# Pinning the order of the ahead-of-time block sums in a one-core decoder layer

## The chip, the cores and the metric

The kernel runs on one core of a Trainium2 chip, in one launch. The metric is the device time of that core in microseconds: 1126.95 us is the median of three runs (1126.46 to 1127.5). Lower is better.

## The reference

One layer of a decoder, in float32, for 256 tokens of width 2048:

- `h = rmsnorm(x)`, then one projection to q, k, v of 16 heads of 128 (8 stick-breaking heads, 8 dilated-window heads with rotary positions);
- attention of each head, its own RMS norm, concatenation, `mix_out = mixed @ w_out`, and `x = x + rmsnorm(mix_out)`;
- `h = rmsnorm(x)`, `u = h @ w_up` (2 x 5504 columns), a causal depthwise convolution of width 3, `y = gelu(gate) * val`, `f = y @ w_down` (5504 rows), and `x = x + rmsnorm(f)`.

For 26 blocks of the last product (13 pairs of row tiles, two column halves) the kernel uses a two-by-two block scheme with fewer products, which needs sums of blocks of `w_down`. These sums depend on the weights alone, so a part of them is made long before `w_down` is multiplied.

## The kernel before, in words

**Chunks.** The weights pass through TensorE in chunks of 128 x 2048 floats, listed in `chunks`: 0 to 7 are v, 8 to 23 q and k of heads 0 to 7 (two chunks a head), 24 to 27 v, 28 to 35 heads 8 to 11, 36 to 39 v, 40 to 47 heads 12 to 15, 48 to 63 the output projection, and from 64 on the up projection. One loop goes over them (L688). Iteration i first calls `ahead(i)`, which loads chunk i+2 in two halves (L78, into one of five `raw` buffers) and splits chunk i+1 into a high part `wh` (ScalarE, L88) and a low part `wl` (VectorE, L93). Then TensorE multiplies chunk i (L101 and L104 for q and k; L134, L135, L138 for v and the output projection). Then `step()` advances every active head by one stage.

**Heads.** A stick-breaking head's second stage makes scores `z` and ends with `spl` on VectorE (L352). Its third stage, one chunk later, multiplies `spl` (L355). A dilated head first rotates q and k (L364 to L368), and its scores (L372, L373) come one chunk later. They are reduced by L378 and L380. `finish_head` normalises a head's output (L316 to L325 on VectorE).

**Block sums ahead of up.** `presum` (L531) is called at the end of iterations 7 to 61 with `tick = i - 7`. At even ticks it stores the sum of pair `tick/2 - 2` to DRAM (L537, from the tile `t13`), and loads the two blocks of pair `tick/2` (L546 into `b12`, two buffers, 256 KB; L548 into `t13`, three buffers, 512 KB). At odd ticks it adds the blocks of pair `(tick-1)/2 - 1` (L542, VectorE). So in the source pair p is loaded in iteration 7+2p, added in iteration 10+2p and stored in iteration 11+2p. The sums are read back in the down projection, after chunk 149.

**What sets the order.** All these loads and stores are issued by SyncE, in one queue with the `raw` loads. A planner orders the instructions of each engine when the program is built. It follows the source as its priority, but lets an instruction pass others that are, by its own model, not ready or waiting for a buffer. `keep_in_program_order` ties one instruction behind the one that the source gave to the same engine just before it. It does not tie the instructions that follow. The helper `pin` (L65) uses it for whole stretches, as around L745 to L843; `presum` does not use it.

Of the kernel before, what the change touches and what calls it, by code (L numbers as in the profile page):

```python
# [13 lines left out]
ALU = mybir.AluOpType  # L14
# [37 lines left out]
def layer_kernel(ctx: ExitStack, tc: tile.TileContext, a, out: bass.AP):  # L52
    nc = tc.nc
    V, A, T, G = nc.vector, nc.scalar, nc.tensor, nc.gpsimd
# [433 lines left out]
    class Down:  # L488
# [42 lines left out]
        def presum(self, tick):  # L531


            pair, odd = divmod(tick, 2)
            if not odd and 0 <= pair - 2 < len(self.presums):
                t13, _, kept = self.summed[pair - 2]
                nc.sync.dma_start(kept, t13)  # L537
            if odd and 0 <= pair - 1 < len(self.presums):
                t13, one, _ = self.summed[pair - 1]
                b12 = one.rearrange("p (o c) -> p o c", o=1).broadcast_to([P, 2, 512])  # L540
                two = t13.rearrange("p (o c) -> p o c", o=2)
                V.tensor_tensor(two, b12, two, op=ALU.add)  # L542
            if not odd and pair < len(self.presums):
                one, two, kept = self.presums[pair]
                b12 = apool.tile([P, 512], F32, tag="b12", name="b12")
                nc.sync.dma_start(b12, one)  # L546
                t13 = apool.tile([P, HALF], F32, tag="t13", name="t13", bufs=3)
                nc.sync.dma_start(t13, two)  # L548
                self.summed.append((t13, b12, kept))

        def load(self, n):
# [394 lines left out]
```

## Time and profile before

| | |
|---|---|
| median of three runs | 1126.95 us |
| the profiled execution's own time | 1126.68 us |
| its span | 1124.8 us |
| TensorE busy | 1106.9 us |
| VectorE busy | 880.2 us |
| ScalarE busy | 659.4 us |
| mean DMA traffic | 229 GB/s |

The span is the stretch from the first to the last recorded instruction. Busy times are sums over an engine's instructions. Matmuls overlap, so their single durations are longer than the distance between two starts. An idle time stands beside the instruction that ended it, with what released that instruction.

### The profile page before, as it was taken

Reading aid. Unit: us, or ns where it says so; the run is one execution under the profiler, and the core shown is the slowest. Engines: PE = TensorE matmul, PEld = TensorE weight load, DVE = VectorE, ACT = ScalarE, POOL = GpSimd, SP = SyncE. Lnnn points to the kernel's source line nnn. Section 1 sums busy time; section 2 is a strip of 40 time slices with the busy share of each in tenths; the row PEclk is TensorE's granted clock in tenths of the full one; section 3 lists DMA queues with packets and bytes.
Section 4 is the critical chain, followed back from the end, with each engine's and each line's share of the span. In section 5 each row is a group of like instructions: output and inputs, shape, how many; then the busy total and the mean of one; then the engine's idle time right before and its main releaser. Section 6 shows DMA issues by size and latency. Waiting matters only on the chain.

```text
span 1124.8 us, 16273 instructions
## 1 busy us (share of the span) xinstructions
PE 1106.9 (98%) x5855; PEld 942.9 (84%) x5855; DVE 880.2 (78%) x1370; ACT 659.4 (59%) x1038; POOL 3.3 (0%) x10
## 2 busy tenths in 40 slices
PE   9999999999999989999999999999999999999997
PEld 6888888888888878888888888888888888888885
DVE  6577776786765478888888888888888798889887
ACT  6656565565654466555555555555555566666664
POOL 0000000000000000000000000000000000000000
PEclk9999999999999999999999999999999999999998
DMA  9978898998645546555555555555555577767776
GB/s 345 340 279 268 295 351 291 321 329 304 220 167 187 192 172 216 188 188 187 188 188 187 187 188 188 187 187 187 188 187 187 162 260 242 254 217 247 243 246 207
DMA packets 74817, 257.79 MB, mean 229 GB/s; under 512 B 8432, under 2 KB 9328, under 8 KB 73968
## 3 DMA queue, kind: packets, MB, share of 16 engines
q1 hardware_dynamic: 74448, 256.68, 68.4%
q8 instruction: 46, 0.75, 0.3%
q14 instruction: 35, 0.29, 0.1%
q10 hardware_dynamic: 288, 0.07, 0.0%
HBM read 238.89 MB, written 17.83 MB: 228 GB/s over the span
## 4 chain that ended last, share of the span: by engine, by line
PE 93%; DVE 2%; DMA 2%; ACT 1%; issue 1%; SPq 0%; DVEq 0%; ACTq 0%
PE mmu L101 28%; PE mmu L104 14%; PE mmqk L101 9%; PE p L590 7%; PE p L589 6%; PE p L588 6%; PE mmqk L104 4%; PE mmo L134 3%; PE mmo L135 3%; PE mmo L138 3%; PE mmv L138 3%; PE mmv L134 3%; PE mmv L135 3%; DVE wl L93 1%; DMA b<-in_w_dn 1%; DMA t<-in_w_dn 1%
## 5 line engine op out<-in xcount | busy, mean ns | idle before, releaser
L88 ACT CAST wh<-raw 128x1024 fp32r<-128x1024 f32 (+1 forms) x413 | 419.3, 1022 | 359.8 <-PE mmu L101 191.3
L93 DVE TENSOR_TENSOR wl<-raw,wh 128x1024 fp32r<-128x1024 f32 (+1 forms) x413 | 486.8, 1186 | 158.6 <-ACT wh L88 156.2
L101 PE MATMUL mmu<-hT,wh 128*128 128x512 f32 x1344 | 340.6, 395 | 0.2 <-ACT wh L88 0.2
L101 PEld LDWEIGHTS mmu<-hT,wh 128*128 128x128 f32 x1344 | 240.8, 188 | 45.0 <-ACT wh L88 0.4
L104 PEld LDWEIGHTS mmu<-hT,wl 128*128 128x128 f32 x1344 | 184.1, 188 | 15.3
L104 PE MATMUL mmu<-hT,wl 128*128 128x256 f32 x1344 | 187.3, 281 | 0.0
L101 PE MATMUL mmqk<-hT,wh 128*128 128x512 f32 x512 | 132.9, 401 | 0.0
L101 PEld LDWEIGHTS mmqk<-hT,wh 128*128 128x128 f32 x512 | 92.0, 188 | 17.2
L104 PEld LDWEIGHTS mmqk<-hT,wl 128*128 128x128 f32 x512 | 69.9, 188 | 5.8
L590 PE MATMUL p<-wl,yp 128*128 128x512 f32 x182 | 71.8, 395 | 0.0
L589 PE MATMUL p<-wh,yp 128*128 128x512 f32 x182 | 71.4, 392 | 0.0
L104 PE MATMUL mmqk<-hT,wl 128*128 128x256 f32 x512 | 71.1, 281 | 0.0
L588 PE MATMUL p<-wh,yp 128*128 128x512 f32 x182 | 70.6, 388 | 0.0
L590 PE MATMUL p<-wl,yt 128*128 128x512 f32 (+1 forms) x140 | 54.1, 387 | 0.0
L589 PE MATMUL p<-wh,yt 128*128 128x512 f32 (+1 forms) x140 | 53.9, 385 | 0.0
L588 PE MATMUL p<-wh,yt 128*128 128x512 f32 (+1 forms) x140 | 53.4, 382 | 0.0
L461 ACT ACTIVATE cv<-u,par 128x256 f32<-128x256 f32 x86 | 51.5, 599 | 2.6 <-DVE u L459 2.5
L134 PE MATMUL mmv<-wh,hT 128*128 128x512 f32 x128 | 51.4, 403 | 0.8 <-ACT wh L88 0.4
L135 PE MATMUL mmv<-wh,hT 128*128 128x512 f32 x128 | 50.7, 396 | 0.2 <-DVE hT L239 0.2
L134 PE MATMUL mmo<-wh,mix 128*128 128x512 f32 x128 | 50.4, 394 | 0.0
L542 DVE TENSOR_TENSOR t<-b,t 128x1024 f32<-128x1024 f32 x26 | 31.8, 1222 | 23.1 <-DMA t<-in_w_dn 23.0
L135 PE MATMUL mmo<-wh,mix 128*128 128x512 f32 x128 | 49.9, 390 | 0.0
(175 smaller groups left out, 1209.5 us busy)
## 6 DMA issues: line engine op xcount, KB each, us to landing
raw<-in_w_up SPq DMA_DIRECT2D x172, 512.0 KB, 4.1
raw<-in_w_qk SPq DMA_DIRECT2D x64, 512.0 KB, 5.4
raw<-in_w_dn SPq DMA_DIRECT2D x60, 512.0 KB, 4.5
raw<-in_w_o SPq DMA_DIRECT2D x32, 512.0 KB, 3.5
raw<-in_w_v SPq DMA_DIRECT2D x31, 512.0 KB, 5.8
t<-in_w_dn SPq DMA_DIRECT2D x26, 512.0 KB, 6.5
t_kept<-t SPq DMA_DIRECT2D x26, 512.0 KB, 6.8
raw<-t_kept SPq DMA_DIRECT2D x26, 512.0 KB, 4.3
```

The lines of the kernel that those rows point to most:

```text
L88: pin(A.copy(wh, raw))
L93: pin(V.tensor_tensor(wl, raw, wh.bitcast(F32), op=ALU.subtract))
L101: T.matmul(ps, wh[:, j * P:(j + 1) * P], h[:, k, :, :], start=(k == 0), stop=False, skip_group_check=True)
L104: T.matmul(ps[:, 0, :], wl[:, j * P:(j + 1) * P], h[:, k, 0, :], start=False, stop=(k == KT - 1), skip_group_check=True)
L134: T.matmul(ps[t], hi[:, k, tc_], ws, start=(first and i == 0 and j == 0), stop=False)
L135: T.matmul(ps[t], lo[:, k, tc_], ws, start=False, stop=False)
L138: T.matmul(ps[t], hi[:, k, tc_], wl[:, j * 512:(j + 1) * 512], start=False, stop=(last and i == len(parts) - 1 and j == n - 1))
L461: A.activation(cv, u, AF.Identity, scale=cw(2), bias=par[:, P_CB + f:P_CB + f + 1])
L542: V.tensor_tensor(two, b12, two, op=ALU.add)
L588: T.matmul(ps, yh, wh[:, cs], start=key not in self.begun, stop=False)
L589: T.matmul(ps, yl, wh[:, cs], start=False, stop=False)
L590: T.matmul(ps, yh, wl[:, cs], start=False, stop=self.left[key] == 0)
```

## The change

The five instructions of `presum` that move or add blocks are each given to `keep_in_program_order`. Nothing is added, removed or resized. Each is tied behind the instruction that the source placed just before it on its engine (SyncE for the three DMAs, VectorE for the addition).

```diff
@@ -534,18 +534,18 @@
             pair, odd = divmod(tick, 2)
             if not odd and 0 <= pair - 2 < len(self.presums):
                 t13, _, kept = self.summed[pair - 2]
-                nc.sync.dma_start(kept, t13)
+                tc.keep_in_program_order(nc.sync.dma_start(kept, t13))
             if odd and 0 <= pair - 1 < len(self.presums):
                 t13, one, _ = self.summed[pair - 1]
                 b12 = one.rearrange("p (o c) -> p o c", o=1).broadcast_to([P, 2, 512])
                 two = t13.rearrange("p (o c) -> p o c", o=2)
-                V.tensor_tensor(two, b12, two, op=ALU.add)
+                tc.keep_in_program_order(V.tensor_tensor(two, b12, two, op=ALU.add))
             if not odd and pair < len(self.presums):
                 one, two, kept = self.presums[pair]
                 b12 = apool.tile([P, 512], F32, tag="b12", name="b12")
-                nc.sync.dma_start(b12, one)
+                tc.keep_in_program_order(nc.sync.dma_start(b12, one))
                 t13 = apool.tile([P, HALF], F32, tag="t13", name="t13", bufs=3)
-                nc.sync.dma_start(t13, two)
+                tc.keep_in_program_order(nc.sync.dma_start(t13, two))
                 self.summed.append((t13, b12, kept))
```

## Rows read from the trace of the kernel before

**Rows 1.** The page: span, and busy time of each engine.
```profile
span 1124.8 us, 16273 instructions
PE 1106.9 (98%) x5855; PEld 942.9 (84%) x5855; DVE 880.2 (78%) x1370; ACT 659.4 (59%) x1038; POOL 3.3 (0%) x10
```
**Rows 2.** Windows: stretch, length, busy times, clock, DMA share, GB/s.
```profile
50.00:100.00 50.00, 50.00 (x296) 43.97 (x295) 37.27 (x63) 29.44 (x56) 0.00 (x0) 1.00 0.79 272
100.00:150.00 50.00, 48.98 (x292) 43.02 (x291) 36.96 (x66) 28.46 (x61) 0.00 (x0) 1.00 0.90 308
150.00:175.00 25.00, 23.36 (x128) 19.69 (x127) 18.86 (x34) 14.76 (x33) 0.00 (x0) 1.00 0.95 335
...
200.00:225.00 25.00, 24.18 (x143) 20.78 (x143) 18.46 (x40) 15.26 (x32) 0.00 (x0) 1.00 0.92 321
225.00:250.00 25.00, 24.57 (x134) 20.94 (x133) 21.29 (x47) 15.59 (x37) 0.00 (x0) 1.00 0.92 323
...
325.00:350.00 25.00, 25.00 (x118) 20.76 (x117) 12.32 (x18) 11.44 (x18) 0.00 (x0) 1.00 0.53 172
```
**Rows 3.** Waits of PE: who waited for whom, total us, times, longest.
```profile
PE z L355 <- DVE spl L352: 2.7, 3, 1.0
...
PE z L372 <- DVE qk L368: 0.9, 2, 0.5
```
**Rows 4.** Timeline of VectorE before an idle time of TensorE.
```profile
155.12 1.23 DVE L542 TENSOR_TENSOR t<-b,t 128x1024 f32<-128x1024 f32 x1 [2.06 <-DMA t<-in_w_dn]
...
159.05 0.55 DVE L352 TENSOR_TENSOR spl<-sp,sph 128x384 fp32r<-128x384 f32 x1
```
**Rows 5.** Timeline of TensorE at that idle time.
```profile
159.65 0.44 PE L355 MATMUL z<-spl,tri 128*128 128x384 f32 x1 [0.91 <-DVE spl L352]
```
**Rows 6.** Timeline of VectorE at a dilated head.
```profile
196.64 1.23 DVE L542 TENSOR_TENSOR t<-b,t 128x1024 f32<-128x1024 f32 x1 [2.41 <-DMA t<-in_w_dn]
197.78 2.35 DVE L93 TENSOR_TENSOR wl<-raw,wh 128x1024 fp32r<-128x1024 f32 x2
200.05 0.42 DVE L726 TENSOR_TENSOR qk<-mmqk,half 128x256 f32<-128x256 f32 x1
```
**Rows 7.** The tile t: additions and the waits before them.
```profile
L542 DVE TENSOR_TENSOR t<-b,t x26: 1212/1225/1228, 53.9 to 283.3; 128x1024 f32<-128x1024 f32 x26
...
  DMA t<-in_w_dn: 23.0, 13
```
**Rows 8.** Timeline of SyncE's issues, start and length.
```profile
40.90 0.42 SPq L548 DMA_DIRECT2D t<-in_w_dn  x1
...
275.71 0.42 SPq L548 DMA_DIRECT2D t<-in_w_dn  x1
```
**Rows 9.** DMA issues: count, KB each, median us to landing.
```profile
raw<-in_w_qk SPq DMA_DIRECT2D x64, 512.0 KB, 5.4
...
t<-in_w_dn SPq DMA_DIRECT2D x26, 512.0 KB, 6.5
```
**Rows 10.** Waits of SyncE's queue.
```profile
SPq L78 <- DVE wl L93: 449.6, 187, 5.8
...
SPq L537 <- DVE m L380: 1.7, 1, 1.7
```
**Rows 11.** Groups by line and shape: busy us, mean ns, idle before.
```profile
L93 DVE TENSOR_TENSOR wl<-raw,wh 128x1024 fp32r<-128x1024 f32 x385 | 467.8, 1222 | 158.3 <-ACT wh L88 156.0 <-PE po L309 1.5
L88 ACT CAST wh<-raw 128x1024 fp32r<-128x1024 f32 x385 | 402.4, 1051 | 353.8 <-PE mmu L101 190.0 <-PE mmqk L101 59.3 <-PE mmo L135 36.0
...
L134 PE MATMUL mmv<-wh,hT 128*128 128x512 f32 x128 | 51.4, 403 | 0.8 <-ACT wh L88 0.4 <-ACT hT L216 0.3
...
L134 PE MATMUL mmo<-wh,mix 128*128 128x512 f32 x128 | 50.4, 394 | 0.0
```
**Rows 12.** Chain of waits, by time: one half chunk of q and k.
```profile
106.32 1.86 PE mmqk L101 x8
108.18 0.95 PE mmqk L104 x8
```

## The prediction

> **What bounds the kernel now.** I read the page first. TensorE is busy for 1106.9 us of the span of 1124.8 us [rows 1], so an edit that adds or removes no matmul can only move the 17.9 us in which TensorE idles. Then I read the windows by stage, to see where that idle time lies. From 50 to 100 us TensorE is busy without a gap. From 100 to 150 it misses 50.00 - 48.98 = 1.02 us, from 150 to 175 it misses 1.64, from 200 to 225 it misses 0.82, and from 225 to 250 it misses 0.43 [rows 2]. That is 3.91 us in the stage in which the block sums run. The other 14 us lie outside that stage, and I leave them as they are.
>
> The waits of TensorE tell who ended these gaps. Three of them, 2.7 us together, ended with `spl` on VectorE, and two, 0.9 us together, with the rotated `qk` [rows 3]. So VectorE was late, though in the same windows it is idle for a sixth to a quarter of the time [rows 2].
>
> The timeline of VectorE shows why. At 155.12 us an addition of `presum` starts after VectorE stood idle for 2.06 us, waiting for the load of `t`. `spl` stands behind it in the queue and starts only at 159.05 [rows 4]. TensorE needs `spl` at L355 and waits 0.91 us for it [rows 5]. The two other gaps before L355 have the same picture, an addition that waits for its load ahead of `spl`. Over the kernel, 13 of the 26 additions waited for their load, 23.0 us in all [rows 7]. The reason is that the planner moved loads and additions up. In the source pair 25 is loaded in iteration 57, in the output projection, but the last load of `t` is issued at 275.71 us, while q and k are still multiplied [rows 8]. Early in the kernel the distance was larger: the first load is issued at 40.90 and the first addition starts at 53.9 us, 13.0 us later [rows 7, 8], where the landing takes 6.5 us [rows 9].
>
> **The change part by part.** The counts stay: 26 additions of 1.225 us [rows 7], and 78 DMA issues. All that moves is when and behind what they stand. The sum is made against the profiled execution's own 1126.68 us, of which 1124.8 are the span; it is 0.27 us under the median of the runs.
>
> *The additions.* Pair p is added at the end of iteration 10+2p, an even one, behind the last VectorE instruction of `step()`. In the stick-breaking stage that instruction is `spl` itself (L352), in the dilated stage L380. So no addition stands ahead of the `spl` of its own iteration. Its load was issued in iteration 7+2p, three chunks earlier. One half chunk takes 1.86 + 0.95 = 2.81 us [rows 12], a chunk 5.62 us without the heads' work, so the distance is about 17 us and the load lands in 6.5 [rows 9]. The 23.0 us of waits should go.
>
> What that gives TensorE: the three gaps before `spl` are 2.7 us. At the second, wait and addition are 2.06 + 1.23 = 3.29 us ahead of `spl`, which started at 159.05 and would start at about 155.8. TensorE was ready at 159.65 - 0.91 = 158.74, and `spl` takes 0.55 us [rows 4, 5], so it would end at about 156.4; what is late next is TensorE's own work, with some 2.4 us to spare. I take all 2.7 us.
>
> The rest of the 3.91, about 1.2 us, are gaps of the dilated heads (0.9 of it before L372). One of them begins with an addition that waits 2.41 us at 196.64; behind it come two `wl`, and `qk` only at 200.05 [rows 6]. Without the wait the rotation would be some 2 us earlier and the gap gone. But in this stage the rotation also shares VectorE with the split of the next chunk, which the change leaves, and the addition itself stays in every second chunk. Bounds: all 1.2 us come back, or none does and new gaps of the same size (0.9 / 2 = 0.45 us [rows 3], at the six of eight dilated heads that don't wait there now) cost 2.7 us. I take half the gain, 0.6 us.
>
> *The loads and stores.* SyncE issues them behind the `raw` loads of chunk i+2, so no `raw` load is put back by a load that passed it. Nothing is added to the queue. I cost it at zero; the cover is the five `raw` buffers. What it costs without the cover is the first rival.
>
> *The pairs that now fall into the output projection.* Loads of pairs 21 to 25 (five) and additions and stores of 19 to 25 (seven) move there. VectorE gets 7 x 1.22 = 8.6 us in some 84 us (15 chunks of about 5.6), in a stage where it is busy 12.32 of 25 us. The DMA engines get 5 x 0.77 + 7 x 0.51 = 7.4 MB (1.29 MB per pair), 90 GB/s on top of 172, which makes 262, less than the 272 at which TensorE ran gapless from 50 to 100 us [rows 2]. Zero; at the worst one addition of 1.22 us slides into the chain between the output projection and up, so 0 to +1.2.
>
> *Matmul speed.* The Trainium skill ("Perfetto Trace Analysis", section "Identifying the Most-Contended Engine") says that TensorE's busy share is not a good measure of how close it is to its limit, so busy time could hide a stretch that lighter DMA traffic gives back. The row that could speak for it is the group of L134: 403 ns a matmul for v, with the DMA share near 0.9, against 394 ns for the output projection at about 0.5 [rows 2, 11]. By that rule the 192 or so matmuls of v behind 100 us would give back 192 x 9 ns = 1.7 us. I take zero in the main sum, since the two have other operands, and keep 1.7 as a rival's price.
>
> Sum: 1126.68 - 2.7 - 0.6 = 1123.4 us.
>
> **The rivals.**
>
> *A held queue (slower).* The store of pair p is tied behind the second `raw` load of chunk 13+2p, and its addition now comes late in iteration 10+2p. SyncE works in order: its waits at L78 for `wl` are 449.6 us, and whatever stands behind waits too. The Trainium skill says the same ("DMA: Bandwidth & Descriptors", section "Anatomy of one DMA — SWDGE (gpsimd) path"): a DMA's semaphore wait is done by the issuing sequencer before dispatch. Before, the store held SyncE for 1.7 us in one case only [rows 10]. A `raw` buffer comes round every five halves, 5 x 2.81 = 14.05 us; landing, `wh` and `wl` take 5.4 + 1.05 + 1.22 = 7.7 [rows 9, 11, 12]. So a hold up to 6.4 us costs nothing, and each us beyond it costs one per pair. From the point where the hold is 7 us, 21 pairs cost 21 x 0.6 = 13 us: 1123.4 + 13 = 1136. Against it: the `raw` loads that follow are not tied behind the store, so the planner may let them pass.
>
> *The idle time comes back elsewhere (no change).* All additions now stand in even iterations, where VectorE also has two `wl`, the norm of one head and the scores of the next. Then `wl`, or the rotation, is late in place of `spl`, for up to the same 3.3 us; or the ties bind little, because the planner already had the source's neighbours. Time 1126.0 to 1127.2, say 1126.6. For it: from 225 to 250 us VectorE is busy for 21.29 of 25 us [rows 2], so any late instruction there is felt. Against it: from 50 to 100 us, where pairs still come at one per two chunks, TensorE has no gap at all [rows 2].
>
> *More than the gaps.* All 3.9 us and the 1.7 us of faster matmuls: 1126.68 - 5.6 = 1121.1.
>
> **How the numbers follow.** The forecast, 1122.5 to 1124.6 with 1123.4 as its value, has 0.58. No change has 0.26, the held queue 0.10, and more than the gaps 0.06. The range runs from 1122.0 (all gaps of the sums gone, with 0.8 us of the faster matmuls) to 1127.4 (the end of no change); it leaves out the held queue and part of the last case, and the likeliest case's own range stands above. A difference under 0.2%, 2.25 us, can hardly be told from no change, so faster means under 1124.7 and slower over 1129.2. Faster takes the forecast and the last case, less a little of the forecast for a second-stage gap that stays: 0.62. Same takes the no-change case and that little: 0.27. Slower has the held queue: 0.11.
>
> **What would show it.** Right: the idle time before L542 falls from 23.0 us to under 3, the waits of TensorE for `spl` vanish, the last load of `t` is issued near 370 us, and the windows from 100 to 250 us show TensorE without a gap. The addition stands behind L352 in the timeline. Wrong: ScalarE's `wh` waits for DMA of `raw` in the q and k stage, or SyncE waits at L537, which is the held queue; or the same sum of gaps with other releasers (`wl`, `qk`), which is the second rival. Output projection and down should keep their gap times.

## The result: faster, by nearly twice what was forecast

| | before | after |
|---|---|---|
| median of the runs compared | 1127.22 us (1126.46 to 1127.52) | 1121.11 us (1120.87 to 1121.22) |
| the profiled execution's own time | 1126.68 us | 1121.22 us |
| its span | 1124.8 us | 1119.3 us |
| ratio, 95% interval | | 0.9946 [0.9929, 0.9964] |

The direction was right. The time lies 2.3 us under the forecast and 0.9 us under the range.

**The page and the windows after.** The first fence is the page's span and busy line, the second the windows that answer to [rows 2] (stretch, length, busy times, clock, DMA share, GB/s).

```profile
span 1119.3 us, 16297 instructions
PE 1105.9 (99%) x5855; PEld 943.1 (84%) x5855; DVE 880.8 (79%) x1370; ACT 659.3 (59%) x1038; POOL 3.3 (0%) x10
```

```profile
100.00:150.00 50.00, 50.00 (x304) 44.44 (x303) 36.48 (x64) 29.70 (x62) 0.00 (x0) 1.00 0.73 251
150.00:175.00 25.00, 25.00 (x134) 21.20 (x133) 17.30 (x33) 15.05 (x34) 0.00 (x0) 1.00 0.73 243
200.00:225.00 25.00, 25.00 (x149) 21.82 (x148) 19.93 (x41) 15.60 (x34) 0.00 (x0) 1.00 0.83 280
225.00:250.00 25.00, 25.00 (x135) 21.22 (x134) 18.57 (x45) 15.53 (x36) 0.00 (x0) 1.00 0.78 260
325.00:350.00 25.00, 25.00 (x116) 20.74 (x115) 15.26 (x20) 11.51 (x19) 0.00 (x0) 1.00 0.80 285
```

Every window of the stage is full on TensorE. The traffic is thinner up to 250 us and thicker in the output projection. TensorE's busy sum fell by 1.0 us although the matmuls are the same, so busy time held a part of what was lost before.

The waits of TensorE after, longest first, hold neither L355 nor L372 of [rows 3]:

```profile
PE mmu L111 <- ACT hT L776: 1.6, 3, 1.0
PE pth L769 <- DVE x L762: 1.6, 1, 1.6
```

**The additions after.** The tile t, to be held against [rows 7] (count, ns, first and last start), VectorE at one iteration, and SyncE's issues beside it.

```profile
L548 SPq DMA_DIRECT2D t<-in_w_dn x26: 422/788/1842, 41.2 to 359.4; - x26
L542 DVE TENSOR_TENSOR t<-b,t x26: 1215/1219/1227, 75.2 to 379.0; 128x1024 f32<-128x1024 f32 x26
...
its engine sat idle before it (us, times) until:
who waited for it (us, times):
```

```profile
115.11 0.55 DVE L352 TENSOR_TENSOR spl<-sp,sph 128x384 fp32r<-128x384 f32 x1
115.58 1.22 DVE L542 TENSOR_TENSOR t<-b,t 128x1024 f32<-128x1024 f32 x1
116.77 1.23 DVE L93 TENSOR_TENSOR wl<-raw,wh 128x1024 fp32r<-128x1024 f32 x1
```

```profile
103.31 0.33 SPq L537 DMA_DIRECT2D t_kept<-t  x1
103.68 0.42 SPq L546 DMA_DIRECT2D b<-in_w_dn  x1
104.16 0.75 SPq L548 DMA_DIRECT2D t<-in_w_dn  x1
105.01 10.54 SPq L78 DMA_DIRECT2D raw<-in_w_qk  x4
```

The 13 waits before L542 are gone: the line of idle times is empty. The addition stands behind `spl`, and the last load of `t` is issued at 359.4 us in place of 275.7. On SyncE a store, a load of `b` and a load of `t` stand together, then four `raw` loads.

**Where the time went.** The 5855 matmuls stand in the same order in both traces. So for each of them I can subtract its start after from its start before, and see where this lead grows. It grows at eight matmuls (each with the one right behind it), all between 115 and 232 us; anywhere else between 20 and 400 us it moves by less than 0.1 us:

```
matmul and its start before     idle shown before it    lead gained there
L355  117.67                          1.02                   1.29
L355  144.96                          none                   0.24
L355  159.65                          0.91                   1.18
L355  174.12                          0.73                   1.01
L372  204.96                          0.52                   0.61
L386  211.16                          0.16                   0.45
L372  218.03                          0.15                   0.41
L372  231.84                          0.43                   0.70
sum                                   3.91                   5.88
```

So the stops really cost 5.9 us, 2.0 more than the idle time that the trace shows. The clock has no part in it: the granted clock is 1.00 from 20 to 400 us in both traces. The first stop shows where the 2.0 us come from. The first fence is TensorE before, the second the same matmuls after.

```profile
116.22 0.42 PE L354 MATMUL z<-sph,tri 128*128 128x384 f32 x1
117.67 0.44 PE L355 MATMUL z<-spl,tri 128*128 128x384 f32 x1 [1.02 <-DVE spl L352]
117.94 0.38 PE L356 MATMUL z<-sp,negones 128*128 128x128 f32 x2
```

```profile
116.57 0.42 PE L354 MATMUL z<-sph,tri 128*128 128x384 f32 x1
116.83 0.34 PE L355 MATMUL z<-spl,tri 128*128 128x384 f32 x1
117.01 0.38 PE L356 MATMUL z<-sp,negones 128*128 128x128 f32 x2
```

From L354 to L356 it takes 1.72 us before and 0.44 after, 1.28 less, where 1.02 idle was shown. After, L355 starts 0.26 us behind L354, while L354's record still runs (0.42). Before, the idle time is counted only from that record's end, so the overlap of 0.16 us is lost besides; and L356 follows L355 at 0.27 us in place of 0.18. A stop shorter than the overlap shows no idle time at all, as at 144.96. The Trainium skill ("TensorE: Matmul & The Clock Gate", section "Single matmul latency") puts the latency of a single bf16 matmul, at the higher clock, at the time of its columns and a constant of about 166 ns. The 0.16 us is of that size, but the trace's ends of matmuls are modelled, so no run here shows that this constant is the cause.

The two ends of the kernel take back a little of the 5.9 us: the first 19 us were 0.35 us longer after, and the rest of the kernel 0.09, which leaves 5.5 us between the spans.

### The profile page after: what moved, and what is told of

It reads as the page before. It is cut to its first block, busy times and chain, and to the rows that moved or that the text cites. A ratio compares the mean times of both kernels' runs of the same rounds, so it can differ in the third digit from the quotient of the medians.

```text
span 1119.3 us, 16297 instructions
## 1 busy us (share of the span) xinstructions
PE 1105.9 (99%) x5855; PEld 943.1 (84%) x5855; DVE 880.8 (79%) x1370; ACT 659.3 (59%) x1038; POOL 3.3 (0%) x10
## 4 chain that ended last, share of the span: by engine, by line
PE 97%; ACT 1%; DMA 1%; DVE 0%; issue 0%; SPq 0%; DVEq 0%
PE mmu L101 28%; PE mmu L104 14%; PE mmqk L101 11%; PE p L589 7%; PE p L588 7%; PE p L590 6%; PE mmqk L104 5%; PE mmv L138 3%; PE mmo L134 3%; PE mmo L135 3%; PE mmo L138 3%; PE mmv L134 3%; PE mmv L135 3%; DMA raw<-in_w_v 1%; PE mmu L111 1%; ACT hT L776 0%
## 5 line engine op out<-in xcount | busy, mean ns | idle before, releaser
L104 PEld LDWEIGHTS mmu<-hT,wl 128*128 128x128 f32 x1344 | 184.1, 188 | 15.3
L104 PE MATMUL mmu<-hT,wl 128*128 128x256 f32 x1344 | 187.4, 282 | 0.0
L104 PEld LDWEIGHTS mmqk<-hT,wl 128*128 128x128 f32 x512 | 69.9, 188 | 5.8
L104 PE MATMUL mmqk<-hT,wl 128*128 128x256 f32 x512 | 71.1, 281 | 0.0
L134 PE MATMUL mmv<-wh,hT 128*128 128x512 f32 x128 | 52.0, 408 | 0.5 <-ACT hT L216 0.3
L134 PE MATMUL mmo<-wh,mix 128*128 128x512 f32 x128 | 50.4, 394 | 0.0
L88 ACT CAST wh<-room 128x1024 fp32r<-128x1024 f32 x26 | 27.3, 1050 | 38.5 <-PE p L589 37.5
```

The source lines that it names most:

```text
L88: pin(A.copy(wh, raw))
L104: T.matmul(ps[:, 0, :], wl[:, j * P:(j + 1) * P], h[:, k, 0, :], start=False, stop=(k == KT - 1), skip_group_check=True)
L134: T.matmul(ps[t], hi[:, k, tc_], ws, start=(first and i == 0 and j == 0), stop=False)
```

## The experiments

Three theories stood. **A**: an addition that waits for its load puts back what stands behind it in VectorE's queue, and the change took these waits away. **B**: the thinner DMA traffic of the stage did it. **C**: the position of the addition behind `spl` did it. The table has what each run gave. "Waits" is VectorE's idle time before the addition (us, times). "Loss" is the time from the 61st matmul (at 19 us) to the first one of up (at 402 us), over that of after; it leaves out the start, which differs from that of after by up to 0.6 us, and what follows, which differs by up to 1.4. The ratio is to runs of before made beside those of the kernel. Each loss is read from one execution. With the transfers alone tied, the addition ahead of step, and the short lead ahead of step, that execution lies over the kernel's median (1123.51, 1123.91 and 1124.95 us), so their losses may be read somewhat high.

| kernel | median us | ratio to before | waits | loss us |
|---|---|---|---|---|
| before | 1127.22 | 1 | 23.0, 13 | 5.91 |
| after | 1121.11 | 0.9946 [0.9929, 0.9964] | none | 0 |
| addition alone tied | 1122.22 | 0.9953 [0.9938, 0.9968] | none | -0.03 |
| transfers alone tied | 1122.17 | 0.9955 [0.9940, 0.9970] | 23.5, 15 | 1.85 |
| addition ahead of step | 1122.38 | 0.9954 [0.9937, 0.9970] | none | 0.86 |
| short lead | 1120.81 | 0.9942 [0.9927, 0.9956] | 1.5, 2 | -0.01 |
| short lead, ahead of step | 1123.39 | 0.9968 [0.9956, 0.9980] | 3.8, 3 | 3.64 |
| no lead | 1121.40 | 0.9949 [0.9934, 0.9964] | 0.2, 1 | -0.03 |
| store held | 1135.63 | 1.0074 [1.0059, 1.0089] | none | 14.34 |
| three stores a sum | 1135.95 | 1.0085 [1.0062, 1.0109] | none | 15.97 |
| late load, ahead | 1125.32 | 0.9984 [0.9973, 0.9995] | 12.9, 6 | 4.65 |
| late load, behind, first | 1122.61 | 0.9961 [0.9949, 0.9974] | 0.2, 1 | 1.15 |
| late load, behind, second | 1123.10 | 0.9962 [0.9950, 0.9974] | 2.9, 5 | 1.97 |
| late load, behind, third | 1125.52 | 0.9982 [0.9972, 0.9991] | 7.9, 3 | 4.23 |

**The addition alone tied.** Against after, the three transfers are free again.

```diff
-                tc.keep_in_program_order(nc.sync.dma_start(kept, t13))
+                nc.sync.dma_start(kept, t13)
...
-                tc.keep_in_program_order(nc.sync.dma_start(t13, two))
+                nc.sync.dma_start(t13, two)
```

> Only the addition is tied; loads and stores are free to move up again. Theory A (an addition that waits for its load stands in VectorE's queue ahead of what TensorE needs next): the additions stay late, behind L352 or L380, so their loads have landed; no wait before L542, TensorE without a gap from 100 to 250 us, 1121.1 us as with all five ties. Theory B (the thinner DMA traffic is what counts, and it needs the ties on the loads): the pace of pairs is still one per two chunks, since the buffers come free with the additions, so B can't differ much either, but loads that pass raw loads would show as waits of wh for raw: 1122 to 1124.

No wait, no stop, and the stage is that of after to 0.03 us. The tied addition is enough: it holds its buffers until its place, and the buffers pace the loads (the last load of `t` stands at 357.9 us). The 1.1 us between the two medians are not in the stage: of the 1.15 us between the two spans, 0.4 lie in the start and 0.7 behind 402 us.

**The transfers alone tied.**

```diff
-                tc.keep_in_program_order(V.tensor_tensor(two, b12, two, op=ALU.add))
+                V.tensor_tensor(two, b12, two, op=ALU.add)
```

> Loads and stores are tied, the addition is not, so the traffic is spread over one pair per two chunks as in the changed kernel, but the planner puts the addition as early as it believes the load landed, often ahead of spl. Theory A: the waits before L542 and the gaps before L355 or L372 come back in part, 0.2 to 0.5 us or more each; 1122 to 1126 us. Theory B (thinner traffic): no gaps, 1121.1 us.

The waits are as long as before, but cost only 1.85 us. By the medians this kernel and the one with the addition alone tied can't be told apart (1122.17 and 1122.22 us); the stage tells them apart, in the one execution read of each. Three fences, all of this kernel: VectorE's wait for the load (us, times, longest), VectorE at one that cost nothing and at one that did, and TensorE behind the second.

```profile
DVE t L542 <- DMA t<-in_w_dn: 23.5, 15, 3.5
```

```profile
166.68 1.23 DVE L542 TENSOR_TENSOR t<-b,t 128x1024 f32<-128x1024 f32 x1 [3.41 <-DMA t<-in_w_dn]
...
170.82 0.55 DVE L352 TENSOR_TENSOR spl<-sp,sph 128x384 fp32r<-128x384 f32 x1
...
194.53 1.23 DVE L542 TENSOR_TENSOR t<-b,t 128x1024 f32<-128x1024 f32 x1 [2.79 <-DMA t<-in_w_dn]
...
202.02 0.68 DVE L368 TENSOR_TENSOR qk<-qk,rot 128x512 f32<-128x512 f32 x1
```

```profile
202.85 0.46 PE L372 MATMUL z<-qk 128*128 128x128 f32 x2 [0.90 <-DVE qk L368]
```

The wait of 3.41 us ended at 166.68, four microseconds ahead of `spl`, and TensorE had no stop. So the sum of the waits says nothing by itself. In before, too, six of the 13 stood ahead of a stop (2.40, 2.06, 1.73, 2.41, 1.95 and 1.11 us, 11.7 in all), and the longest one, 3.15 us at 133.28, ahead of none that shows idle time.

**The addition ahead of step.** All tied, but the addition is made before the heads' work of its iteration.

```diff
-        step()
+        down.presum(i - 7, moves=False) if 7 <= i < 62 else None; step()
```

> All five are tied, the addition is called before step() and so stands ahead of sp and spl of its own iteration, with the same three chunks between load and addition. Theory A (the wait counts): no wait before L542, VectorE is delayed by 1.22 us at most and spl still comes in time; 1121.1 us, at most one or two gaps (1122). Theory C (the place ahead of spl alone counts): gaps at L355 and L372 as before, 1124 to 1127 us.

No addition waits, and position alone costs 0.86 us, all of it behind 200 us, in the dilated heads, and none before L355. That is a seventh of what before lost: C is a small part of it.

**A short lead.** The addition and the store come two iterations earlier than in after, so an addition follows its load at one iteration.

```diff
-            if not odd and 0 <= pair - 2 < len(self.presums):
-                t13, _, kept = self.summed[pair - 2]
+            if not odd and 0 <= pair - 1 < len(self.presums):
+                t13, _, kept = self.summed[pair - 1]
...
-            if odd and 0 <= pair - 1 < len(self.presums):
-                t13, one, _ = self.summed[pair - 1]
+            if odd and 0 <= pair < len(self.presums):
+                t13, one, _ = self.summed[pair]
```

Two more kernels vary this. One makes the addition ahead of `step()` with the short lead; one adds each pair at the end of the very iteration that loads it (no lead). The three expectations, in this order:

> All five are tied, the addition stands behind spl as in the changed kernel, but each pair is added one iteration after its load instead of three (and stored one after that), so the load has 6 to 8 us to land in 5.5. Theory A: VectorE waits before L542 again (some us in all), but spl is not behind it; what is behind is wl of the next chunk, with slack; 1121 to 1123 us. If the wait alone counts wherever it stands: the gaps of the kernel before come back, 1124 to 1127 us.

> All five tied; the addition is called before step(), so it stands ahead of sp and spl, and only one iteration after its load. Theory A (a wait of VectorE for the load, standing ahead of what TensorE needs next): if the load has landed as it had with one iteration of lead behind step() (waits of 1.5 us in all), only the place costs, as in the run with the addition before step() and three chunks of lead, where the q, k and v stage lost 0.7 us: about 1121.5 to 1122.5 us. If waits of 1 to 2 us show before L542, gaps before L355 come back, each idle time plus about 0.27 us: 1123 to 1126. Theory C (place alone): the same as with the long lead.

> All five tied; each pair is added at the end of the iteration that loads it (7+2p), so VectorE waits 3 to 5 us for the load in that iteration (26 times, some 80 to 110 us in all), with the two wl of the next chunk behind the addition, and spl of the next iteration later. DMA traffic and pace as in the changed kernel. Theory A: TensorE stops at many of these, where the wait is longer than the slack of wl (about 2 to 3 us): 10 to 25 stops of 0.5 to 2 us plus 0.27 each, 1130 to 1160 us. Theory B (traffic): no loss, 1121 us.

Behind `step()` the short lead is as good as the long one, and so is no lead at all, where the addition stands in the iteration of its own load. SyncE runs an iteration or more ahead of TensorE, so a load that the source puts beside its addition is issued early enough: with no lead, the load of `t` issued at 107.58 us is added at 119.00, while loads of `t` landed in 4.6 to 8.4 us. That part of what I expected (waits of 80 us and more, 1130 to 1160 us) was wrong, and with hardly a wait left these two kernels don't test what a wait behind `spl` costs. Ahead of `step()`, the short lead leaves three waits, and two of them stop TensorE. VectorE and TensorE of that kernel:

```profile
237.55 1.22 DVE L542 TENSOR_TENSOR t<-b,t 128x1024 f32<-128x1024 f32 x1 [2.14 <-DMA t<-in_w_dn]
238.70 0.68 DVE L366 TENSOR_TENSOR qk<-qk,cosR 128x512 f32<-128x512 f32 x1
...
241.04 0.68 DVE L368 TENSOR_TENSOR qk<-qk,rot 128x512 f32<-128x512 f32 x1
```

```profile
241.77 0.49 PE L372 MATMUL z<-qk 128*128 128x128 f32 x2 [1.67 <-DVE qk L368]
```

One wait of 2.14 us right ahead of the rotation stops TensorE for 1.67 us shown, and its lead falls by 1.93. The two stops of this kind make up 3.0 of the 3.64 us; the rest is the position's, as in the kernel before.

**Late loads.** In six pairs of the stick-breaking heads ScalarE issues the load of `b12` late, in the iteration of the addition. In the first kernel the addition stands ahead of the head's work, in the others behind `spl` with the two `wl` of the next chunk tied behind it, and the load is issued ahead of the heads' work of the iteration, behind `e` (L346), or behind `sph` (L350). The diff has two of the changed lines of the first kernel. The expectations follow in this order; `forced_ahead` and `forced_behind` in them are the first kernel and the first of those behind `spl`.

```diff
-                tc.keep_in_program_order(nc.sync.dma_start(b12, one))
+                if pair not in FORCED: tc.keep_in_program_order(nc.sync.dma_start(b12, one))
...
-        step()
+        late_add[0] = i % 2 == 0 and (i - 10) // 2 in FORCED; late_b(i); down.presum(i - 7, moves=False) if late_add[0] else None; step()
```

> After, but in the pairs 1 to 6 (iterations 12 to 22, stick-breaking heads) the one-block load of the addition is issued late, by ScalarE right behind the first work of that iteration, and the addition stands ahead of the head's work in step(), with hv and spl kept behind it on VectorE. So six waits are made by force, each standing ahead of the spl that TensorE needs next. Theory A (a wait costs where it stands ahead of what TensorE needs next): the addition waits some 4 to 5 us, spl ends some 3 to 4.5 us later than TensorE is ready for L355, six stops at L355, each its shown idle and 0.27 us more, +18 to +28 us against after, about 1139 to 1149. Rival (a wait costs TensorE the same wherever in VectorE's queue it stands): forced_ahead and forced_behind lose alike per us waited. Rival (a wait costs nothing, the gain came from the order of the transfers): about 1121, as after.

> The same six late loads by ScalarE in the same iterations, but the addition stays where after has it, behind spl (L352), and the two wl of the next chunk are kept behind it. Theory A: the addition waits some 0.5 to 2 us, and behind it stand only the two wl, which TensorE needs some 2 to 3 us later; no stop at L355, none or a few short stops elsewhere, 1121 to 1125. Rival (a wait costs wherever it stands): loses per us waited as much as forced_ahead, so 6 x 0.5 to 2 us, 1124 to 1133, and the stops are spread over whatever comes next.

> As forced_behind (six additions at their place behind spl, the two wl of the next chunk kept behind them), but ScalarE issues the one-block load later, behind the last pass of e (L346), so that the addition has to wait, by the landings seen so far some 2 to 3 us, as long as in forced_ahead (1.5 to 3.2 us). Theory A (what counts is what stands behind the wait): only wl is put back, by the length of the wait, and TensorE needs it about that much later; 0 to 1 us lost per pair, 1121 to 1126, none of it before L355 or L329. Rival (a wait costs wherever it stands): 12 to 18 us of waits lose at the rate of forced_ahead (4.2 us of TensorE time for 12.9 us waited), 4 to 6 us, 1125 to 1127. The two overlap at 1125 to 1126; then the place of the stops decides.

> The same with the load issued one step later, behind sph (L350): the addition waits some 3.5 to 5 us, and wl comes that much later. Its matmuls on TensorE are ordered somewhat otherwise (heads' matmuls between those of wh and wl). Theory A: the wait is now longer than the time by which wl is ahead (2 to 3 us), so each pair stops TensorE at its first matmul of wl for 1 to 2.5 us, 6 to 15 us in all, 1127 to 1136; the stops stand at L104 or L138 with wl as releaser. Rival (a wait costs in proportion, 0.33 us per us waited): 21 to 30 us of waits, 7 to 10 us, 1128 to 1131, spread over other stops.

Waits made by force bring stops back. The sizes were missed: the loads landed sooner than I had reckoned, so the waits were 1.5 to 3.2 us in place of 4 to 5, and the stops came at L329 and not at L355: `on` (L325) stands behind the wait as well, and at the first of them the planner had put five matmuls of `wh` between L329 and L354. So 4.65 us were lost where 18 to 28 were expected. The first kernel's waits on VectorE and TensorE, and VectorE at the first of them:

```profile
DVE t L542 <- DMA b<-in_w_dn: 12.9, 6, 3.2
```

```profile
PE pt L329 <- DVE on L325: 2.8, 3, 1.3
```

```profile
87.01 1.23 DVE L542 TENSOR_TENSOR t<-b,t 128x1024 f32<-128x1024 f32 x1 [3.17 <-DMA b<-in_w_dn]
...
90.14 0.61 DVE L325 TENSOR_SCALAR on<-po,rr 128x128 f32<-128x128 f32 x2
```

Behind `spl` is no shelter either. In the third kernel of that place (VectorE, then TensorE) a wait of 4.79 us puts back the two `wl`, and TensorE stops at its first matmul of `wl`:

```profile
131.63 1.23 DVE L542 TENSOR_TENSOR t<-b,t 128x1024 f32<-128x1024 f32 x1 [4.79 <-DMA b<-in_w_dn]
132.77 2.35 DVE L93 TENSOR_TENSOR wl<-raw,wh 128x1024 fp32r<-128x1024 f32 x2
```

```profile
134.04 1.21 PE L104 MATMUL mmqk<-hT,wl 128*128 128x256 f32 x8 [1.12 <-DVE wl L93]
```

4.79 us of wait gave 1.12 us of shown stop. From the first matmul of `wh` to the first of `wl` it is 1.27 us more than in after, so `wl` had some 3.5 us to spare (an estimate, from these numbers). Only three of the six late loads made the addition wait here, 7.9 us in all where 21 to 30 were expected; two of the three put a stop at L104, as theory A had it. The first two kernels of that place settle little: their waits were too short (0.2 and 2.9 us), and they lost 1.15 and 1.97 us, mostly at one stop near 160 us, at L138, where the order of v's matmuls differs from after. That the loss is one rate per microsecond waited is refuted all the same: it is 0.08 with the transfers alone tied (1.85 / 23.5), 0.36 with the late load ahead (4.65 / 12.9) and 0.96 with the short lead ahead of step (3.64 / 3.8).

**Three stores a sum.** Each sum is stored to two more places, which brings the traffic of the stage back to the level of before and beyond it.

```diff
-                tc.keep_in_program_order(nc.sync.dma_start(kept, t13))
+                for to in (kept, *(x[(pair - 2) // NPAIR, (pair - 2) % NPAIR] for x in self.again)): tc.keep_in_program_order(nc.sync.dma_start(to, t13))
```

> All five tied; each sum is stored two times more, to DRAM that nobody reads, so the traffic of the q, k and v stage rises by 1.05 MB per two chunks, some 75 GB/s, to 320 to 335 GB/s and a DMA share above 0.9, as much as the kernel before had there. Theory B (thinner traffic is what the change brought): gaps and later raw loads come back, 1124 to 1128 us. Theory A: the additions still follow their loads by three chunks, so no wait before L542 and at most one or two gaps; 1121 to 1123 us.

Its windows, and TensorE's longest waits:

```profile
100.00:150.00 50.00, 50.00 (x304) 44.45 (x303) 36.29 (x63) 29.71 (x63) 0.00 (x0) 1.00 0.88 318
150.00:175.00 25.00, 25.00 (x132) 21.18 (x132) 17.43 (x33) 14.88 (x34) 0.00 (x0) 1.00 0.89 326
175.00:200.00 25.00, 25.00 (x136) 21.38 (x135) 14.91 (x22) 11.78 (x20) 0.00 (x0) 1.00 0.97 352
200.00:250.00 50.00, 49.82 (x278) 42.81 (x277) 38.88 (x84) 31.31 (x69) 0.00 (x0) 1.00 0.99 363
250.00:300.00 50.00, 44.93 (x237) 38.09 (x237) 29.73 (x55) 22.15 (x45) 0.00 (x0) 0.97 0.86 311
```

```profile
PE mmqk L101 <- ACT wh L88: 5.4, 3, 2.6
PE mmo L134 <- ACT wh L88: 5.0, 3, 1.8
```

The time, 1135.95 us, lies far over both cases of the expectation. From 100 to 175 us the traffic is about what before had [rows 2] and TensorE has no gap, where before lost 2.7 us shown. So B is refuted at the level of before. Nor is thin traffic enough: the short lead ahead of step has 252 GB/s from 225 to 250 us, where its longest stop lies. Up to the last matmul of v, at 258 us, this kernel is 0.3 us behind after, counted from the 61st matmul; nearly all its loss comes later, behind stretches of 352 to 363 GB/s, and the releaser of its longest stops is `wh`. The 0.97 in the last window's row is the granted clock: behind a stop of 1.86 us at 260.41 it is 0.50 (1.2 GHz) from 262 to 265 us, and that stop cost 3.6 us.

Whether the traffic or the three stores that stand in SyncE's queue made `wh` late stays open. The holds there are at most 7.7 us (119 us in all), shorter than holds that cost nothing in the next kernel, which speaks for the traffic. The Trainium skill ("DMA: Bandwidth & Descriptors", section "Where 436 GB/s comes from") puts the limit of a core's memory at about 358 GB/s; the windows of 352 and 363 GB/s, at DMA shares of 0.97 and 0.99, lie about there. But from 350 to 375 us this kernel moved 379 GB/s at a share of 1.02, so the trace shows no limit at that figure.

**The store held.** Here the store of a sum stands right behind its addition in the source, with the `raw` loads of the next iteration tied behind it.

```diff
-            nc.sync.dma_start(raw, src[:, lo:lo + n])
+            (tc.keep_in_program_order if tied[0] else lambda ins: ins)(nc.sync.dma_start(raw, src[:, lo:lo + n]))
...
+            if odd and 0 <= pair - 1 < len(self.presums):
+                t13, _, kept = self.summed[pair - 1]
+                tc.keep_in_program_order(nc.sync.dma_start(kept, t13))
```

> The queue's hold made longer: the store is called right behind its addition (iteration 10+2p instead of 11+2p), and in iterations 7 to 61 the raw loads are tied too, so they can't pass it. SyncE meets the store one chunk earlier, so it is held some 2 + 6 = 8 us a pair instead of 2 us (40.8 us in 20 holds, longest 4.4, in the changed kernel). By the prediction's rival (slack 6.4 us, then one us per us): 26 pairs lose about 1.5 to 2 us each, 1155 to 1175 us, with wh waiting for raw loads. If the queue's hold is covered more deeply than that: 1121 to 1125 us.

SyncE's waits at the store after (L537) and in this kernel (L542), then TensorE's longest stop there:

```profile
SPq L537 <- DVE t L542: 40.8, 20, 4.4
...
SPq L537 <- DVE rq L151: 12.3, 6, 2.2
```

```profile
SPq L542 <- DVE t L539: 165.0, 18, 16.6
...
SPq L542 <- DVE rq L149: 36.7, 4, 9.4
```

```profile
270.18 2.12 PE L101 MATMUL mmqk<-hT,wh 128*128 128x512 f32 x5 [2.60 <-ACT wh L88]
```

After holds SyncE for up to 4.4 us at a store, 26 times, and pays nothing.

With about 9 us of hold per pair (238 us in all) the loss is 14.3 us, well under the 34 us and more that I expected by the rival, and well over the 4 of the other case. It is not spread over the pairs. The first five holds, of 9.4 to 16.6 us, cost nothing, and neither did those of 8.3 to 9.4 us from 199 to 245 us. But 8.5 us were lost at two stops, where `wh` waited for `raw`: at 270.18 us (2.60 shown, 4.4 lost) behind a hold of 12.7 us, and at 349.49 (2.34 shown, 4.1 lost) behind one of 13.5. A part of these two is the clock: behind the stops the granted clock is 0.50 (1.2 GHz) from 271 to 274 and from 350 to 352 us, where it was 1.00 before them, and the five matmuls in the row above take 2.12 us, where eight took 2.11 at 261.72. The rest are smaller stops, 3.6 us of them between 135 and 200 us, which ended with `spl`, `wl` and `wh`; why is not shown.

## Why the prediction was right and where it failed

- **The mechanism held.** The order on SyncE and the place of the addition on VectorE came out as written: the 23.0 us of waits went to none, `spl` and `qk` left the list of TensorE's waits, and the windows from 100 to 250 us are full. The experiments bear it out from both sides: without the waits the loss is gone (addition alone tied), with waits made anew ahead of what TensorE needs next a loss is back (3.64 us with the short lead ahead of step, 4.65 with the late load ahead).
- **The step that failed is the size of the gain.** "I take all 2.7 us" priced a stop at the idle time shown, as did the premise that the edit "can only move the 17.9 us in which TensorE idles": 2.0 of the 5.9 us stood in no idle time. The three stops at L355 cost 1.29 + 1.18 + 1.01 = 3.5 us, and a fourth, which shows no idle time, 0.24. That is 1.0 us short.
- **"I take half the gain, 0.6 us"** was short by more. All four gaps of the dilated heads went, and they cost 0.61 + 0.45 + 0.41 + 0.70 = 2.2 us. I had reckoned that the split of the next chunk and the addition itself would keep half of it. They don't: with both still in place after, the waits for `qk` are gone. Both together, 3.3 forecast and 5.9 measured, are the miss.
- **The transfers at zero**: right. SyncE's waits at L537, which I had named as a sign of being wrong, did come, 53 us in 26 holds. But none is over 4.4 us, under the slack of 6.4 us that the rival named, and TensorE lost nothing. The slack itself was set too small: in the kernel with the store held, holds of 9.4 us and more cost nothing, and 14.3 us were lost where the rival's rule gives 71 ((9.14 - 6.4) x 26).
- **The pairs in the output projection at zero**: right. From 325 to 350 us the traffic is 285 GB/s and TensorE has no gap.
- **"More than the gaps" had the right time, 1121.1, by luck.** Its 3.9 us of gaps did come, but the 1.7 us of faster matmuls did not. The matmuls of v at L134 did not become faster: their group (busy us, mean ns, idle before) has 408 ns after, against 403 in [rows 11], and the lead over before does not grow in them.

```profile
L134 PE MATMUL mmv<-wh,hT 128*128 128x512 f32 x128 | 52.0, 408 | 0.5 <-ACT hT L216 0.3 <-ACT wh L88 0.2
```

  What busy time hid was the lost overlap at each stop. The sentence from the Trainium skill pointed to the right place, busy time; the row by which I tested it, a mean duration, could not show it, the distance between starts at a stop could.
- **The range** had its low end at all gaps as shown and half of that rival. Priced by starts, "all gaps gone" is 1126.68 - 5.9 = 1120.8, and it should have reached there. The last load of `t`, expected near 370 us, was issued at 359.4.

What stays open: why before's start and tail differ by 0.4 us from after's (the start varies so between profiles of other kernels too), and what in the planner puts a freed addition where its wait is cheap in one kernel and dear in another.

No kernel is shown to beat after. The short lead's median is 0.3 us lower, its stage is the same to 0.01 us, and the difference lies in the start.

## What to carry to other kernels

An instruction that waits for a transfer in an in-order queue costs by what stands behind it and how much room that has, not by its length alone; so put it behind the urgent work and give it a load that is issued early. Price a stop of TensorE from start to start of the matmuls around it, in a stretch with the stop and one without, and look at the granted clock behind it; the shown idle time here was a third too small, and short stops did not show at all. Where the work to be delayed also holds buffers, tying that one instruction can pace its transfers as well.

## What was not expected of the hardware

- A stop of TensorE cost 0.1 to 0.3 us more than its shown idle time (eight stops: 3.91 shown, 5.88 real).
- Behind two stops of 2.60 and 2.34 us (store held) and one of 1.86 us (three stores) the granted clock fell from 1.00 to 0.50 for some three us, and they cost 4.4, 4.1 and 3.6 us. Behind one of 2.64 us at 276.09 (three stores) it stayed at 1.00, and that one cost 2.9.
- Holding SyncE's queue at a store for up to 4.4 us per pair was free, and so were holds of 9.4 to 16.6 us up to 130 us; two of 12.7 and 13.5 us later were each followed by a stop of TensorE.
- With three stores a sum, DMA shares of 0.88 and 0.89 (318 and 326 GB/s) left TensorE without a gap; the gaps began behind 0.97 and more (352 to 363 GB/s).
